# An encoder block's output projection in seven half-size products per half of K, with its stages passed through DRAM

## The chip, the cores and the metric

One core of a Trainium2 chip runs the whole program. The metric is device microseconds of one execution. TensorE (PE) multiplies matrices into PSUM, eight banks of 128 x 512 float32. VectorE (DVE), ScalarE (ACT) and GpSimd (POOL) work on tiles of 128 partitions. Each engine takes its instructions in order. All transfers are issued by SyncE (SP), in order too, and run on 16 DMA engines.

## The reference

```python
h = rmsnorm(x, norm_w[l])                              # x: (1, 1024, 2048)
proj = jnp.einsum('bsd,de->bse', h, w_in[l])           # 2048 -> 5632
q_a, k_a, v_a, g_a, q_r, k_r, v_r, g_r = jnp.split(proj, points, axis=-1)
attn = windowed_attention(q_a, k_a, v_a, sink, rel_bias)   # 16 heads of 64, 4 kv heads, blocks of 128, +-128 tokens
attn = rmsnorm(attn, attn_out_norm_w[l]) * jax.nn.silu(g_a)
qr, kr = rotary(q_r), rotary(k_r) * RET_KEY_DIM ** -0.5
ret = bidirectional_retention(qr, kr, vr, decay_fwd, decay_bwd)   # 8 heads, chunks of 128
ret = head_groupnorm(ret, ret_gn_w[l]) * jax.nn.silu(g_r)
mixed = jnp.concatenate([attn, ret], axis=-1)          # (1, 1024, 2048)
x = x + jnp.einsum('bse,ed->bsd', mixed, w_out[l])     # 2048 -> 2048
return rmsnorm(x, final_norm_w)
```

## The kernel before

Every float32 operand of a large matmul is split into a high and a low part of the type that TensorE takes in one pass (`split`: ScalarE writes the high part, another engine the rest), and each product is three matmuls: high x high, high x low, low x high.

**Input projection.** `UNITS` lists 22 blocks of 256 columns: `ka`, `va` (keys and values of the attention), `qa` 0 to 3, `ga` and `gr` (gates), and for each pair of retention heads `qk` and `vr`. A unit is 16 steps over k, each with 12 matmuls of 128x512 (24 of 128x256 for `va` and `vr`) into four PSUM banks; at the last k the banks are evicted (`evac`) into tiles. The weights of two k-steps come in one tile, loaded a pair ahead (`w_load`) and split a pair ahead (`w_split`).

**What runs between.** After each bank's matmuls of a k-step the code calls `point()`, which lets generators emit a piece of other work. `jobs` holds the attention of four head groups (`attn_job`), then the retention of four pairs (`ret_job`); `aux` holds the setup, the row norms (`sumsq`), the relative-bias rows (`bias_rows`), the decays, and the work that follows a unit (gates, rotation). The order that the generators give is the program's order on every engine and on SP. `drain` runs a generator to a named end at once.

**Tiles.** `t2` is a pool of six tiles of 128x512, `t4` of five of 128x1024. Gates (`gd`), attention and retention outputs (`md`), keys, bias rows (`bd`) and decays go through DRAM already; q, the values and the rotated q and k of the retention stay on the chip.

**Output projection.** K is the 2048 mixed features. Blocks are 512 tokens (`hf`) x 512 columns (`cb`), four banks of 128 tokens, 16 steps over k with 12 matmuls of 128x512: 8 blocks. Rows of `md` are loaded, weighted, split into `hT` (`mixed_row`). `evac_out` adds x to a bank, `finish_out` applies the final norm to four tiles of 128 tokens, `finish_last` to the last.

```python
                for b in range(4):
                    p = banks[b]
                    mh, ml = row[:, 128 * b : 128 * b + 128], row[:, 512 + 128 * b : 512 + 128 * b + 128]
                    T.matmul(p, mh, wh, start=(k == 0), stop=False)
                    T.matmul(p, mh, wl, start=False, stop=False)
                    T.matmul(p, ml, wh, start=False, stop=(k == NK - 1))
```

Of the kernel before, what the change touches and what calls it, by code (L numbers as in the profile page):

```python
# [21 lines left out]
W_IN_TILES = 22 * 8  # L22

UNITS = [("ka", 0), ("va", 0), ("ga", 0), ("qa", 0)]
UNITS += [("ga", 1), ("gr", 0), ("qa", 1), ("ga", 2), ("gr", 1), ("qa", 2), ("ga", 3), ("qa", 3), ("gr", 2)]
for _p in range(4):
    UNITS += [("qk", _p), ("vr", _p)]
UNITS += [("gr", 3)]
TOK_MAJOR = ("va", "vr")
# [3 lines left out]
def hybrid_block(ctx: ExitStack, tc: tile.TileContext, a: dict, out: bass.AP):  # L33
# [5 lines left out]
    md = dram.tile([2048, S], F32, name="md")  # L39
    kd = dram.tile([256, S], F32, name="kd")  # L40
    vd = dram.tile([4, 128, 8, 64], F32, name="vd")
    bd = dram.tile([16, 128, 512], F32, name="bd")
    br = dram.tile([16, 512], F32, name="br")
    dd = dram.tile([8, 128, 128], F32, name="dd")
    qdd = dram.tile([4, 128, 2, 128], F32, name="qdd")
    rbd = dram.tile([128, S], F32, name="rbd")

    cp = ctx.enter_context(tc.tile_pool(name="const", bufs=1))
    wp = ctx.enter_context(tc.tile_pool(name="w", bufs=2))
    hp = ctx.enter_context(tc.tile_pool(name="h", bufs=1))  # L50
    ps = ctx.enter_context(tc.tile_pool(name="ps", bufs=1, space=PSUM))
    com_ctx = ctx.enter_context(ExitStack())
    com = com_ctx.enter_context(tc.tile_pool(name="com", bufs=1))
    ph_ctx = ctx.enter_context(ExitStack())
    att = ph_ctx.enter_context(tc.tile_pool(name="att", bufs=1))

    hT = hp.tile([128, 32, 1024], F32R, name="hT")
# [8 lines left out]
    rb = cp.tile([128, S], F32, name="rb")  # L66
# [4 lines left out]
    phase = [att]  # L71
# [5 lines left out]
    def t4(dt=F32):  # L77
        return com.tile([128, 1024], dt, tag="t4", name=nm("t4_"), bufs=5)

    def t2():  # L80
        return com.tile([128, 512], F32, tag="t2", name=nm("t2_"), bufs=6)
# [7 lines left out]
    def pS():  # L89
        return psum("S", 2)  # L90

    def pT():
        return psum("T", 1)

    def pO():
        return psum("O", 1)

# [10 lines left out]
    def rsqrt_small(v, k, tag, bufs=1):  # L108
        y = small(k, tag + "y", bufs)
        t = small(k, tag + "t", bufs)  # L110
        tt(G, y, v, mhalf[:, :k], ALU.pow)
        tt(V, t, v, y, ALU.mult)
        tt(V, t, t, y, ALU.mult)
        V.tensor_scalar(t, t, -0.5, 1.5, ALU.mult, ALU.add)
        return y, t

    def col_to_rows(col, dst):
        for h in range(2):
            p = pS()
            for i in range(4):  # L120
                c = 4 * h + i
                T.matmul(
                    p[:, 128 * i : 128 * i + 128],
                    col[:, c : c + 1].to_broadcast([128, 128]),
                    ident,
                    start=(i == 0),
                    stop=True,
                    skip_group_check=True,
                )
            A.copy(dst[:, 512 * h : 512 * h + 512], p)  # L130


    wraw, wsp, wide = {}, {}, [None]

    def w_src(i):
        return a["w_in"][i] if i < W_IN_TILES else a["w_out"][(i - W_IN_TILES) % 64]

    n_w = W_IN_TILES + 112

    def w_load(i):  # L140
        if i < n_w and i not in wraw:
            r = wp.tile([128, 512], F32, tag="wr", name=f"wr{i}")
# [3 lines left out]
    def w_split(i):  # L146
        if i < n_w and i not in wsp:
            if wide[0] is None or i % 2:
                hi = wp.tile([128, 512], F32R, tag="wh", name=f"wh{i}")
                lo = wp.tile([128, 512], F32R, tag="wl", name=f"wl{i}")  # L150
            else:
                hi = wide[0].tile([128, 512], F32R, tag="wh", name=f"wh{i}", bufs=2)
                lo = wide[0].tile([128, 512], F32R, tag="wl", name=f"wl{i}", bufs=2)
            r = wraw.pop(i)
            split(hi, lo, r, G if i < W_IN_TILES else V)
            wsp[i] = (hi, lo)


    jobs, aux = deque(), deque()
# [20 lines left out]
    pt, due, pace, apace = [0], [0], [3], [2]  # L180

    def point():
        pt[0] += 1
        if pt[0] >= due[0]:
            due[0] = max(due[0], pt[0] - 1) + pace[0]
            pump(jobs, 1)
        if pt[0] % apace[0] == 0:
            pump(aux, 1)

    def drain(queue, until):  # L190
        while until not in done:
            if until is None and not queue:
                return
# [7 lines left out]
    xraw = {}  # L201
# [9 lines left out]

    def x_split(k):
        if k < NK:
            r = xraw.pop(k)
            n = nw[:, k : k + 1]
            for z in (0, 512) if k == 0 else (0,):
                sl = slice(z, z + 512) if k == 0 else slice(0, 1024)
                if k:
                    A.activation(hT[:, 2 * k, sl], r[:, sl], AF.Copy, scale=n)
                else:  # L220
                    V.tensor_scalar(hT[:, 2 * k, sl], r[:, sl], n, None, ALU.mult)
                stt(V, hT[:, 2 * k + 1, sl], r[:, sl], n, hT[:, 2 * k, sl].bitcast(F32), ALU.mult, ALU.subtract)

    def setup():
# [5 lines left out]
        V.tensor_scalar(ew, ew, 0.5, None, ALU.mult)  # L230
# [3 lines left out]
    def bias_rows():  # L234
# [11 lines left out]
        SP.dma_start(br, bt[:16, :])  # L246
        yield
        reps = {}
        for h in range(16 + 1):
            if h < 16:  # L250
                reps[h] = t2()
                b0 = br[h : h + 1, 0:512]
                SP.dma_start(reps[h], bass.AP(tensor=b0.tensor, offset=b0.offset, ap=[[0, 128], [1, 512]]))
            if h:
                SP.dma_start(bd[h - 1], reps.pop(h - 1))
            yield
        done.add("bias")

    def sumsq():
# [20 lines left out]
        for _ in range(7):  # L280
            yield
        col_to_rows(rcol, rb)
        done.add("rb")
        yield

    def decay():
# [37 lines left out]
        ab = t2()  # L324
        SP.dma_start(ab, a["masks"])
        yield
        yield
        for h in range(8):
            o = t2() if h % 4 == 0 else o
            oo = o[:, 128 * (h % 4) : 128 * (h % 4) + 128]  # L330
            V.tensor_scalar(oo, ab[:, 0:128], lg[:, h : h + 1], None, ALU.mult)
            stt(V, oo, ab[:, 128:256], lg[:, 8 + h : 9 + h], oo, ALU.mult, ALU.add)
            A.activation(oo, oo, AF.Exp)
            V.tensor_scalar(oo, oo, 0.125, None, ALU.mult)
            SP.dma_start(dd[h], oo)
            yield
        for p in range(4):
            o = t2() if p % 2 == 0 else o
            oo = o[:, 256 * (p % 2) : 256 * (p % 2) + 256]
            A.activation(oo[:, 0:128], ab[:, 256:384], AF.Exp, scale=lg[:, 16 + p : 17 + p])  # L340
            A.activation(oo[:, 128:256], ab[:, 384:512], AF.Exp, scale=lg[:, 20 + p : 21 + p])
            SP.dma_start(qdd[p], oo.rearrange("p (d i) -> p d i", d=2))
            yield
        done.add("decay")


    def k_post(tiles):
        while "rb" not in done:
            yield
        for b, t in enumerate(tiles):  # L350
            et, hf = b // 2, b % 2
            stt(V, t, t, 0.125, rb[:, 512 * hf : 512 * hf + 512], ALU.mult, ALU.mult)
            SP.dma_start(kd[128 * et : 128 * et + 128, 512 * hf : 512 * hf + 512], t)
            yield
        done.add("k")

    def gate_post(tiles, et0, key, late=None):
        for b, g in tiles:
            et, hf = b // 2, b % 2

            e = t2()
            A.activation(e, g, AF.Tanh, scale=0.5)
            yield
            stt(V, g, e, 1.0, g, ALU.add, ALU.mult)
            c = et0 + et
            if late is None:
                SP.dma_start(gd[128 * c : 128 * c + 128, 512 * hf : 512 * hf + 512], g)
            else:
                yield
                while ("ret", 3) not in done:  # L370
                    yield
                late(et, hf, g)
            yield
        done.add(key)

    def rope_post(p, tiles, rq, rk):
        for hf in range(2):
            cs, sn = (retp[0].tile([128, 512], F32, tag="mr", name=nm("cs"), bufs=2) for _ in range(2))
            SP.dma_start(cs, a["cos"][:, 512 * hf : 512 * hf + 512])
            SP.dma_start(sn, a["sin"][:, 512 * hf : 512 * hf + 512])  # L380
            yield
            for et, dst in ((0, rq), (1, rk)):
                t = tiles[2 * et + hf]
                sh = t2()
                V.stream_shuffle(sh, t, [i ^ 1 for i in range(32)])
                tt(V, t, t, cs, ALU.mult)
                yield
                tt(V, sh, sh, sn, ALU.mult)
                tt(V, dst[:, 512 * hf : 512 * hf + 512], t, sh, ALU.add)
                yield  # L390
        done.add(("rope", p))
# [4 lines left out]
    def attn_job(g, q_tiles, start):  # L396
        pace[0] = (4.5, 4.5, 3, 3.8)[g]
        kh, kl, vs = t4(F32R), t4(F32R), t4(F32R)
        bias = {}
# [5 lines left out]

        load_bias(0)
        load_bias(1)
        for hf in range(2):
            kr = t2()
            for d2 in range(2):  # L410
                SP.dma_start(kr[64 * d2 : 64 * d2 + 64, :], kd[64 * g : 64 * g + 64, 512 * hf : 512 * hf + 512])
            split(kh[:, 512 * hf : 512 * hf + 512], kl[:, 512 * hf : 512 * hf + 512], kr)
        yield
        vr = t2()
        SP.dma_start(vr, vd[g].rearrange("p t d -> p (t d)"))
# [666 lines left out]
```

## Time and profile before

| what | value |
|---|---|
| median of three runs | 1583.9 us (1580.77 to 1584.82) |
| the profiled execution | 1581.46 us, its span 1579.7 us |
| TensorE busy | 1539.7 us, 97% |
| VectorE, ScalarE, GpSimd busy | 798.9, 525.2, 414.1 us |
| DMA | 171.76 MB, mean 109 GB/s |
| mean granted TensorE clock | 0.994 |

Times in the views are microseconds from the span's start. A group's row gives line, engine, operation, tiles written and read, shape, count, then busy time, mean of one in ns, and the engine's idle time before it with what ended it. In a chain, "start, length, what" stand in a row. TensorE's matmuls are pipelined: each is shown longer than the distance to the next.

### The profile page before, as it was taken

The page shows a single profiled execution, that of the slowest core. Times are in us where ns is not written, and L with a number is a line of the kernel's source. Part 1 is how long each engine was busy: PE and PEld are TensorE (multiplying, and loading weights), DVE is VectorE, ACT ScalarE, POOL GpSimd, SP SyncE. Part 2 cuts the span into 40 slices and gives each one's busy share as a digit, 9 for nine tenths or more (in the row PEclk, how much of TensorE's full clock was granted, in tenths as well). Part 3 has the DMA queues.
Part 4 walks back from the last instruction along what each step waited for, and adds up shares of the span by engine and source line. Part 5 has one row for each costly group of instructions (what it writes and reads, how often), then busy time and mean ns, then how long its engine had stood idle before and what let it go on. Part 6 is the DMA issues. An engine that isn't in the chain of part 4 may idle for free.

```text
span 1579.7 us, 22620 instructions
## 1 busy us (share of the span) xinstructions
PE 1539.7 (97%) x8338; PEld 1327.6 (84%) x8338; DVE 798.9 (51%) x1888; ACT 525.2 (33%) x1186; POOL 414.1 (26%) x435
## 2 busy tenths in 40 slices
PE   8979999999999999999999999999999999999997
PEld 6968888888888888888998998998988888888886
DVE  5511156644656478466534825735567463463323
ACT  5412145543554356456410111111123243433310
POOL 2212223332334334334331423323322000320000
PEclk9989999999999999999999999999999999999999
DMA  8774313131213123212231321312222565675423
GB/s 299 246 248 125 104 43 92 51 114 45 84 56 114 48 60 94 73 48 83 54 113 41 107 61 50 111 41 67 88 89 91 186 205 151 180 247 139 127 61 113
DMA packets 111020, 171.76 MB, mean 109 GB/s; under 512 B 17932, under 2 KB 39436, under 8 KB 110781
## 3 DMA queue, kind: packets, MB, share of 16 engines
q1 hardware_dynamic: 110908, 170.32, 35.3%
q8 instruction: 65, 1.06, 0.3%
q14 instruction: 47, 0.38, 0.1%
HBM read 138.26 MB, written 32.01 MB: 108 GB/s over the span
## 4 chain that ended last, share of the span: by engine, by line
PE 82%; DVE 8%; DMA 4%; issue 3%; ACT 1%; POOL 1%; SPq 0%; POOLq 0%; ACTq 0%; DVEq 0%
PE psM L817 14%; PE psM L818 14%; PE psM L819 14%; PE psM L811 3%; PE psM L812 3%; PE psM L810 3%; PE psM L900 3%; PE psM L901 3%; PE psM L899 3%; PE psT L502 2%; DMA t<-br 1%; DVE t L102 1%; PE psS L900 1%; PE psS L899 1%; PE psS L901 1%
## 5 line engine op out<-in xcount | busy, mean ns | idle before, releaser
L817 PE MATMUL psM<-hT,wh 128*128 128x512 f32 x1088 | 443.0, 407 | 14.9 <-ACT t L741 8.7
L819 PE MATMUL psM<-hT,wl 128*128 128x512 f32 x1088 | 425.9, 392 | 2.0 <-POOL wl L99 2.0
L818 PE MATMUL psM<-hT,wh 128*128 128x512 f32 x1088 | 426.2, 392 | 0.0
L99 POOL TENSOR_TENSOR wl<-wr,wh 128x512 fp32r<-128x512 f32 x176 | 234.5, 1333 | 583.7 <-ACT wh L105 570.7
L105 ACT CAST wh<-wr 128x512 fp32r<-128x512 f32 x288 | 178.5, 620 | 568.7 <-PE psM L818 226.4
L817 PEld LDWEIGHTS psM<-hT,wh 128*128 128x128 f32 x1088 | 205.7, 189 | 53.6 <-ACT t L741 8.9
L819 PEld LDWEIGHTS psM<-hT,wl 128*128 128x128 f32 x1088 | 204.9, 188 | 47.3 <-POOL wl L99 2.4
L818 PEld LDWEIGHTS psM<-hT,wh 128*128 128x128 f32 x1088 | 206.1, 189 | 37.5 <-DVE hT L102 0.7
L810 PE MATMUL psM<-wh,hT 128*128 128x256 f32 x640 | 183.5, 287 | 1.4 <-ACT wh L105 1.4
L811 PE MATMUL psM<-wl,hT 128*128 128x256 f32 x640 | 181.9, 284 | 2.4 <-POOL wl L99 2.4
L812 PE MATMUL psM<-wh,hT 128*128 128x256 f32 x640 | 181.8, 284 | 0.0
L99 DVE TENSOR_TENSOR wl<-wr,wh 128x512 fp32r<-128x512 f32 x112 | 84.1, 751 | 130.8 <-ACT wh L105 130.7
L811 PEld LDWEIGHTS psM<-wl,hT 128*128 128x128 f32 x640 | 123.4, 193 | 3.0 <-POOL wl L99 2.8
L810 PEld LDWEIGHTS psM<-wh,hT 128*128 128x128 f32 x640 | 123.5, 193 | 2.5 <-ACT wh L105 1.6
L812 PEld LDWEIGHTS psM<-wh,hT 128*128 128x128 f32 x640 | 123.4, 193 | 0.0
L450 DVE CUSTOM_DVE_ANT_0 P<-psS,bias,nsink 128x384 f32<-128x384 f32 (+1 forms) x128 | 74.3, 580 | 91.7 <-PE psS L444 91.3
L454 ACT ACTIVATE P<-P,nmx 128x384 f32<-128x384 f32 (+1 forms) x128 | 75.6, 590 | 92.1 <-DVE nmx L450 90.7
L900 PE MATMUL psM<-wl,hT 128*128 128x512 f32 x256 | 100.0, 391 | 0.6 <-DVE wl L99 0.5
L899 PE MATMUL psM<-wh,hT 128*128 128x512 f32 x256 | 100.0, 391 | 0.0
L901 PE MATMUL psM<-wh,hT 128*128 128x512 f32 x256 | 99.7, 389 | 0.0
L99 POOL TENSOR_TENSOR acc<-acc,sq 64x128 f32<-64x128 f32 x112 | 54.9, 490 | 156.2 <-ACT sq L483 148.1
L99 DVE TENSOR_TENSOR t<-psM,rb 128x512 f32<-128x512 f32 x64 | 42.2, 685 | 93.4 <-PE psM L819 93.2
(200 smaller groups left out, 2259.6 us busy)
## 6 DMA issues: line engine op xcount, KB each, us to landing
wr<-in_w_in SPq DMA_DIRECT2D x176, 256.0 KB, 2.7
wr<-in_w_out SPq DMA_DIRECT2D x112, 256.0 KB, 2.8
t<-in_x SPq DMA_DIRECT2D x16, 512.0 KB, 6.9
mr<-md SPq DMA_DIRECT2D x32, 256.0 KB, 3.0
xr<-in_x SPq DMA_DIRECT2D x32, 256.0 KB, 3.9
out<-y SPq DMA_DIRECT2D x32, 256.0 KB, 3.0
t<-in_xT SPq DMA_DIRECT2D x15, 512.0 KB, 5.8
gd<-t SPq DMA_DIRECT2D x28, 256.0 KB, 2.4
```

The source lines that it names most:

```text
L99: eng.tensor_tensor(o, x, y, op)
L105: A.copy(o_hi, x)
L454: A.activation(x[:, :W], x[:, :W], AF.Exp, bias=nmx[:, c : c + 1], scale=-1.0, accum_out=sums[:, c : c + 1])
L810: T.matmul(po, hh[:, sl], wh[:, ws], start=first and z == 0, stop=False, skip_group_check=True)
L811: T.matmul(po, hh[:, sl], wl[:, ws], start=False, stop=False, skip_group_check=True)
L812: T.matmul(po, hl[:, sl], wh[:, ws], start=False, stop=last, skip_group_check=True)
L817: T.matmul(p, wh[:, ws], hh[:, sl], start=first, stop=False)
L818: T.matmul(p, wh[:, ws], hl[:, sl], start=False, stop=False)
L819: T.matmul(p, wl[:, ws], hh[:, sl], start=False, stop=last)
L899: T.matmul(p, mh, wh, start=(k == 0), stop=False)
L900: T.matmul(p, mh, wl, start=False, stop=False)
L901: T.matmul(p, ml, wh, start=False, stop=(k == NK - 1))
```

## The change

**The output projection** is now four problems: half of K (`f`) x half of the columns (`u`, 1024). In each, the mixed features are a matrix of 2 x 2 quarters of 512 tokens x 512 features, the weights 2 x 2 quarters of 512 x 512, and the four quarters of the result come from seven products of one (sums or differences of) feature quarters with one of weight quarters (Strassen's scheme in the form with shared sums). A product is 4 k-steps x 4 token tiles x 3 matmuls of 128x512 in four banks; a product's banks are added to tiles of the result, some products run on in the banks of another.

- `w_combine` makes the four weight combinations of each (`f`, `u`, k) during the input units and stores them in `wd`.
- `premix` reads a row of `md` and its gate from `gd`, weights it and writes it back to `md`; `combine` reads four quarters, makes four combinations and stores them in `cd`. Those of `f` = 0 are made during units 15 to 20, those of `f` = 1 during the first seven products. `c_load` and `c_split` bring the operand rows into `H`, seven tiles that hold the normed input before.
- `e_load` brings x (for `f` = 0) or the partial result `yd` (for `f` = 1) into tiles, `e_done` stores the partial result or squares the final one, `finish` and `finish_last` apply the final norm.

**The stages** pass through DRAM: q's parts (`qsd`), both halves of the attention's sum (`mpd`, added by `attn_sum`), rotated q and k (`rqk`), values (`vrd`). The units' order is new (all gates last), a store is issued some points after its data is made (`store`), the sink is a further column of the exponential's row, and gates use SiLU instead of tanh. **The bias rows** are copied for one head group at a time (`bias_copies`), group 0 before unit 2, the rest from unit 5 on.

```diff
+W_OUT = [
+    (f, u, p, j)
+    for f in range(2)
+    for u in range(2)
+    for p in ((0, 1, 2, 3, 6, 4, 5) if f and u else (0, 1, 2, 3, 4, 6, 5))
+    for j in range(4)
+]
...
+    def t2(dt=F32):
+        return out_of(com, [128, 512], dt, "t2", NT2)
...
-        for h in range(16 + 1):
+    def bias_copies(g):
+        yield ready("rows")
+        for h in range(4 * g, 4 * g + 4):
+            r = t2()
+            b0 = br[h : h + 1, 0:512]
+            SP.dma_start(r, bass.AP(tensor=b0.tensor, offset=b0.offset, ap=[[0, 128], [1, 512]]))
+            yield
+            yield
+            store(bd[h], r, r, (lambda: done.add(("bias", g))) if h % 4 == 3 else None, 1)
+            yield
...
+    def premix(kk):
+        for hf in range(2):
+            sl = slice(512 * hf, 512 * hf + 512)
+            r, g = t2(), t2()
+            SP.dma_start(r, md[128 * kk : 128 * kk + 128, sl])
+            SP.dma_start(g, gd[128 * kk : 128 * kk + 128, sl])
...
+            yield
+            yield
+            stt(V, r, r, ew[:, kk : kk + 1], g, ALU.mult, ALU.mult)
+            store(md[128 * kk : 128 * kk + 128, sl], r, r, (lambda: done.add(("pre", kk))) if hf else None, 2)
...
+    def combine(f, j):
+        yield ready(("pre", 8 * f + j), ("pre", 8 * f + 4 + j))
+        q = [t2() for _ in range(4)]
+        for n in (0, 2, 3, 1):
+            SP.dma_start(q[n], q_mix(f, j, n))
...
+        c = t2()
+        tt(V, c, q[0], q[2], ALU.subtract)
+        store(cd[f, 2, j], c, c, None, 2)
...
+    for j in range(4):
+        for kk in (8 + j, 12 + j):
+            aux.append((premix(kk), None))
+        if j:
+            aux.append((combine(1, j - 1), None))
+    aux.append((combine(1, 3), None))
+    apace[0] = 1.3
...
+        def products(j, t):
+            wh, wl = wsp[W_STD + 4 * n + j]
+            hh, hl = (H[p][:, j, 512 * z + 128 * t : 512 * z + 128 * t + 128] for z in range(2))
+            fresh = j == 0 and p in (0, 1, 3)
+            T.matmul(banks[t], hh, wh, start=fresh, stop=False, skip_group_check=True)
+            T.matmul(banks[t], hh, wl, start=False, stop=False, skip_group_check=True)
+            T.matmul(banks[t], hl, wh, start=False, stop=(j == 3), skip_group_check=True)
+
+        def stream(i):
+            w_split(i + 1)
+            w_load(i + 2)
+            w_load(i + 3)
```

How the instructions stand now, at three places. The transfers on SP ahead of the eviction of unit 1 (`va`, stored to `vd`), before: copies of bias rows out of `br` into `t2` tiles and on to `bd`, with the weights (`wr`) between.

```order
L255 DMA bd<-t_65_891 128x512
L253 DMA t_66_906<-br 128x512
L253 DMA t_67_921<-br 128x512
L255 DMA bd<-t_66_906 128x512
L255 DMA bd<-t_67_921 128x512
L143 DMA wr_943<-in_w_in 128x512
L253 DMA t_69_957<-br 128x512
L255 DMA bd<-t_68_936 128x512
L253 DMA t_70_972<-br 128x512
L745 DMA vd<-t_71_981 128x4x64
```

The same place now: the last of group 0's four copies, the decays' columns (`dc`, `jc`), and loads and stores of weight combinations (`wc`, `wd`).

```order
L113 DMA bd<-t_123_930 128x512
L370 DMA t_127_988<-br 128x512
L113 DMA wd<-wc_852 128x512
L244 DMA wc_1053<-in_w_out 128x512
L412 DMA dc_1058<-in_ret_decay_bwd 64x4x1 x2
L417 DMA jc_1065<-in_jcol 128x2
L113 DMA wd<-wc_928 128x512
L113 DMA bd<-t_127_988 128x512
L228 DMA wc_1177<-in_w_out 128x512
L113 DMA vd<-t_128_1002 128x4x64 x2
```

Twelve of the sixteen copies have left this place; the decays' gathers, which stood behind the copies, stand among the last of them.

SP at the start of the output projection, before: weights (`wr`), feature rows from `md` (`mr`), x (`xr`).

```order
L143 DMA wr_12202<-in_w_out 128x512
L143 DMA wr_12227<-in_w_out 128x512
L893 DMA fw<-in_final_norm_w 128x2048
L143 DMA wr_12251<-in_w_out 128x512
L946 DMA xr_12333<-in_x 128x512
L143 DMA wr_12272<-in_w_out 128x512
L946 DMA xr_12342<-in_x 128x512
L946 DMA xr_12351<-in_x 128x512
L714 DMA mr_12404<-md 128x512
L143 DMA wr_12295<-in_w_out 128x512
```

Now, in the third product: weights (`e`, from `wd`), `premix` (L845, L846, its store L113 to `md`), `combine` (L867, stores to `cd`), the partial result (`yd`).

```order
L113 DMA md<-t_2191_12257 128x512
L214 DMA e_2200_12297<-wd 128x512
L867 DMA t_2201_12303<-md 128x512
L867 DMA t_2203_12305<-md 128x512
L113 DMA md<-t_2196_12278 128x512
L867 DMA t_2204_12306<-md 128x512
L867 DMA t_2202_12304<-md 128x512
L214 DMA e_2207_12324<-wd 128x512
L113 DMA yd<-acc_12108 128x512
L113 DMA cd<-t_2208_12330 128x512
L113 DMA cd<-t_2203_12305 128x512
L113 DMA yd<-acc_12110 128x512
```

Between two loads of weights stood one or two other transfers; now there are four or five.

TensorE in the output projection, before, one k-step's last tile and the next step's first: a tile has 16 such steps.

```order
L899 MATMUL psM_11927<-wh_12128,hT 128x512
L900 MATMUL psM_11927<-wl_12129,hT 128x512
L901 MATMUL psM_11927<-wh_12128,hT 128x512
L899 MATMUL psM_11924<-wh_12154,hT 128x512
L900 MATMUL psM_11924<-wl_12155,hT 128x512
L901 MATMUL psM_11924<-wh_12154,hT 128x512
```

Now, in the first product: the same three matmuls, operand rows from `H`, and the scheduler has put a tile's second k-step ahead of the next tile's first.

```order
L1210 MATMUL psMa_12116<-wh_12035,h0r 128x512
L1211 MATMUL psMa_12116<-wl_12036,h0r 128x512
L1212 MATMUL psMa_12116<-wh_12035,h0r 128x512
L1210 MATMUL psMa_12116<-wh_12132,h0r 128x512
L1211 MATMUL psMa_12116<-wl_12133,h0r 128x512
L1212 MATMUL psMa_12116<-wh_12132,h0r 128x512
```

The form of a matmul is unchanged; a product takes 48 of them, and there are 28 products.

More of the change, by code (lines that the diff above doesn't have):

```diff
@@ L70, in hybrid_block @@
     cnt = [0]
[L71 removed]
+    phase = [stp]
     def nm(p):
@@ L191, in drain @@
         while until not in done:
-            if until is None and not queue:
-                return
+            if not queue:
+                flush(True)
+                if until is None or until in done:
+                    return
             g, _ = queue[0]
@@ L407, in attn_job @@
         load_bias(1)
[L408 to L417 removed]
+        q_load(0)
```

1082 lines of the change are left out of this document (617 added, 465 removed).

## The prediction

> **What bounds the kernel now.** I read the page's busy shares and the chain first, then the steps of the matmuls in time, then what TensorE waits for, then stretches of the span with the DMA share beside them.
>
> ```profile
> span 1579.7 us, 22620 instructions
> PE 1539.7 (97%) x8338; PEld 1327.6 (84%) x8338; DVE 798.9 (51%) x1888; ACT 525.2 (33%) x1186; POOL 414.1 (26%) x435
> PE 82%; DVE 8%; DMA 4%; issue 3%; ACT 1%; POOL 1%; SPq 0%; POOLq 0%; ACTq 0%; DVEq 0%
> ```
>
> TensorE is busy for all but 40 us, and it holds 82% of the chain that ended last: what it need not do comes off the time, as long as it is fed. Busy matmuls overlap, so the mean of one (389 ns) is not its price. The price is the distance of the starts:
>
> ```profile
> 1308.38 0.39 PE L899 MATMUL psM<-wh,hT 128*128 128x512 f32 x1
> 1308.61 0.39 PE L900 MATMUL psM<-wl,hT 128*128 128x512 f32 x1
> ...
> 1309.74 0.39 PE L899 MATMUL psM<-wh,hT 128*128 128x512 f32 x1
> ```
>
> Six starts in 1.36 us: 0.227 us for one 128x512 matmul. What TensorE waits for, and where (in the rows of stretches the columns are length, busy time of PE, PEld, DVE, ACT and POOL with counts, granted clock, DMA share, GB/s):
>
> ```profile
> PE psM L817 <- ACT t L741: 8.7, 1, 8.7
> PE psM L817 <- DVE hT L221: 6.2, 1, 6.2
> ...
> 35.00:40.00 5.00, 5.00 (x24) 4.14 (x23) 2.22 (x4) 2.93 (x4) 1.72 (x1) 1.00 1.03 409
> 160.00:820.00 660.00, 653.92 (x3455) 560.92 (x3454) 363.88 (x942) 301.08 (x778) 232.52 (x280) 1.00 0.26 75
> 820.00:1217.00 397.00, 390.54 (x2538) 351.38 (x2537) 218.20 (x545) 58.77 (x103) 117.06 (x94) 1.00 0.24 75
> 1217.00:1293.00 76.00, 75.52 (x349) 62.42 (x348) 45.09 (x94) 30.47 (x57) 2.86 (x2) 1.00 0.57 184
> 1400.00:1420.00 20.00, 19.91 (x88) 16.15 (x87) 16.53 (x39) 3.83 (x7) 2.02 (x3) 1.00 0.88 288
> 92.00:116.00 24.00, 12.99 (x83) 12.09 (x82) 1.75 (x4) 2.70 (x6) 3.08 (x3) 0.79 0.91 281
> 40.00:60.00 20.00, 20.00 (x121) 17.89 (x119) 11.96 (x15) 9.62 (x16) 4.07 (x3) 1.00 0.98 346
> 1217.00:1570.00 353.00, 352.44 (x1568) 291.00 (x1566) 157.19 (x286) 112.14 (x215) 27.68 (x25) 1.00 0.51 156
> 1570.00:1579.70 9.70, 0.09 (x1) 0.00 (x0) 3.19 (x11) 2.24 (x6) 0.92 (x1) 0.69 0.32 108
> ```
>
> So the idle time is the head (6.2), one hole near 105 us, 6.1 us in the attention stretch (160 to 820), 6.5 in the retention stretch (820 to 1217), under 1 us in the output projection, and 9.7 after the last matmul. The output projection uses half of the DMA engines' time. The rows 40:60 and 35:40 show how fast they go when they are asked for everything: 346 GB/s over 20 us, 409 over 5.
>
> **The products.** Before: 8 blocks x 16 k x 4 tiles x 3 = 1536 matmuls of 128x512. After: 4 (half of K, half of the columns) x 7 products x 4 k x 4 tiles x 3 = 1344. All other matmuls stay in number and shape. 192 x 0.227 = **-43.6 us**. That is all that arithmetic can give; the sums and differences that pay for it go to VectorE and the DMA engines.
>
> **The start.** The 16 bias rows are now copied for one head group (4 rows) before the attention opens, the rest later. Before, all 16 went through the six `t2` tiles in one go, and the eviction of `va` waited for a free one:
>
> ```profile
> 84.37 5.39 DMA t<-br
> 90.14 4.11 DMA t<-br
> ...
> 103.86 4.82 DMA t<-br
> 108.70 4.60 DMA bd<-t
> 113.48 0.85 ACT t L741 x2
> 114.37 0.80 PE psM L817
> ```
>
> and in the timeline (start, duration, line, tiles):
>
> ```profile
> 114.97 0.63 PE L818 MATMUL psM<-hT,wh 128*128 128x512 f32 x1
> 115.39 0.63 PE L819 MATMUL psM<-hT,wl 128*128 128x512 f32 x1
> ```
>
> Row 92:116 has 24.0 - 13.0 = 11.0 us of idle TensorE, and then matmuls start 0.42 to 0.43 us apart (114.97, 115.39) instead of 0.227; I count 12 of them up to 119.7, 2.4 us. Together 13.4. With 4 copies between `br` and `vd` in place of 16 the hole goes; late next is the decay's column of small gathers, which lands after 6 to 7 us:
>
> ```profile
> dc<-in_ret_decay_bwd SPq DMA_DIRECT2D x2, 1.0 KB, 7.0
> jc<-in_jcol SPq DMA_DIRECT2D x1, 1.0 KB, 6.6
> ```
>
> VectorE waits for it just ahead of the same eviction: 0 to 4 us, I take 1.4. Sum **-12** (-13 to -9).
>
> **Attention and retention.** q, k, v, the attention's sums and the rotated q and k now go through DRAM, so the engines do less per step. Per head step VectorE loses half of the scaling (L462), the q parts and the sum of the two halves:
>
> ```profile
> L462 DVE TENSOR_SCALAR P<-P,sums 128x384 f32<-128x384 f32 x96 | 46.1, 523 | 1.5
> L99 DVE TENSOR_TENSOR qj<-t,qj 64x256 fp32r<-64x256 f32 x64 | 30.5, 476 | 1.9
> L99 DVE TENSOR_TENSOR u<-psO,sq 64x256 f32<-64x256 f32 x64 | 26.6, 415 | 61.6 <-ACT sq L479 60.1 <-POOL wl L99 0.7 <-issue 0.6
> ```
>
> About 0.26 + 0.24 + 0.21 of some 2.3 us. TensorE's 12.6 us of idle time in these two stretches are what less work there can win; new are loads that an engine can wait for in order, with 42 to 69 DMAs in each of the units 2 to 7 where there were 14 to 34. At 60% use of the DMA engines a load lands in about the time of the rows below (3 to 4 us) and stands two to three steps ahead of its use. I take **-4** (-10 to +15). The 64 differences of weights (0.69 us each, L947's price below) run beside the input projection on a VectorE that row 160:820 has at 55%; one more table load for the gates' SiLU is 1.3 us on ScalarE behind banks that VectorE frees. Both cost nothing as long as the DMAs land; with that cover gone they are in the upper bound.
>
> **The output projection's feed.** This is the term that decides. The combinations of the first half of K are made during the last input units, those of the second half during the first seven products: 8 rows x 2 halves x 3 DMAs (read `md` and `gd`, write `md`) = 48, four combinations x 8 = 32, weights 28, x tiles in 20, partial y out 16, the last gates 4: 148 DMAs of 256 KB, 38.8 MB, in 7 x 48 x 0.227 = 76.3 us of matmuls. That asks for 509 GB/s; row 1217:1293, the same 76 us before, has 184.
>
> ```profile
> wr<-in_w_out SPq DMA_DIRECT2D x112, 256.0 KB, 2.8
> mr<-md SPq DMA_DIRECT2D x32, 256.0 KB, 3.0
> xr<-in_x SPq DMA_DIRECT2D x32, 256.0 KB, 3.9
> L964 SPq DMA_DIRECT2D out<-y x28: 332/332/454, 1399.5 to 1565.3; - x28
> L947 DVE TENSOR_TENSOR y<-psM,xr 128x512 f32<-128x512 f32 x19 | 12.6, 687 | 32.4 <-PE psM L928 15.4 <-DMA xr<-in_x 9.5 <-PE psM L901 7.5
> ```
>
> The weights of a step stand in the same SP queue as all these, three k-steps (8 us) ahead, so TensorE follows the queue. Issuing is not the limit (148 x 0.33 = 49 us). At 409 GB/s the 38.8 MB take 95 us, at 346 they take 112, at the 281 of row 92:116 they take 138. I take 346, the longest stretch near a full share: 112 - 76 = **+36** (19 to 62). The second seven products carry 95 DMAs, 24.9 MB: 72 us at 346, 76 by row 1400:1420 scaled to a full share (288 / 0.88 = 327). That just fits: **+3** (0 to 12). The last fourteen carry little.
>
> The Trainium skill, "DMA: Bandwidth & Descriptors", Specifications, gives about 358 GB/s as the HBM limit of one core; by that figure the stretch would take 108 us, an estimate 4 us below my term. The 409 of row 35:40 stands above that figure, so the measurement decides, and my lower bound stays.
>
> **Change of stage and tail.** At the end of the last input unit ScalarE and VectorE split rows whose loads were issued one k-step (12 x 0.227 = 2.7 us) before and land in 3.0; the banks of the first product are freed by VectorE behind them: **+4** (0 to 10). At the end, three scalings of the third tile on ScalarE (0.71 us each, L994) stand ahead of the last tile's squares:
>
> ```profile
> L994 ACT ACTIVATE y<-y,fy 128x512 f32<-128x512 f32 x2 | 1.3, 714 | 2.0 <-DVE fy L989 2.0
> ```
>
> **+2** on the 9.7 (0 to 8).
>
> **Sum.** The profiled execution took 1581.5 us for its span of 1579.7. 1581.5 - 43.6 - 12 - 4 + 36 + 3 + 4 + 2 = 1566.9. The median of the three runs, 1583.9, is 2.4 above that execution, so 1569 beside the median.
>
> **Rivals.**
>
> *The feed is hidden.* The queue reaches the best rate (409), or the splits' order lets part of it go early: feed +19 or less, the rest as above: 1552; with the smaller terms at their good ends 1537. For it: 409 and a share of 1.03 in row 35:40. Against: those are loads alone, and a third of the new traffic is stores. Chance 0.2.
>
> *Round trips through six tiles (slower).* `premix` and `combine` take all their tiles from `t2`, six of them: load, VectorE, store, and the next load waits until the store has landed. That is the chain of 84 to 113 us, where six tiles gave 281 GB/s at a share of 0.91 and one DMA in the chain took 4 to 5 us. Place: the first seven products. 38.8 MB at 281 is 138 us, feed +62: 1595. Without the feed the sum is -50.6, so it decides from 127 us for the seven products (306 GB/s) on: above, the change gains nothing. For it: the same tiles and the same pattern; against: weights and x tiles have buffers of their own and fill the queue. Chance 0.2.
>
> *Half clock.* If the waits come in pieces as long as the hole at 105 us, matmuls go on at 0.43 us: 336 x 0.43 = 144 us, feed +68: 1601. For it: rows 114.97 and 115.39; against: the need is spread, about 1.3 us of waiting for each of 28 k-steps, and a 6.2 us head is the only other long wait. Chance 0.07. The Trainium skill, "TensorE: Matmul & The Clock Gate", Part 1, says the same: after an idle window of some 3.4 us the clock halves until it has been busy as long. The trace agrees (0.43 after 8.7 us).
>
> *The change does not cut the work*, because what it takes off TensorE comes back as reloads or extra passes: TensorE's instructions are 192 fewer in the order, so 0.03.
>
> **How the numbers follow.** My forecast (feed between the rates 409 and 306) has 0.5, its own range 1552 to 1582. Less than 0.3% (4.8 us) can hardly be told from no change in this kernel, whose three runs span 4.0 us. Faster (below 1579): all of the hidden case, most of mine, 0.66. Same: the upper end of mine and the lower of the round trips, 0.13. Slower: 0.21. The range 1540 to 1597 leaves out the best of the hidden case and the half clock.
>
> **What would show it.** Right: first seven products in 105 to 120 us, DMA share above 0.9 there, TensorE waiting for ScalarE's or GpSimd's split of weights that wait for the DMA; fourteen last products at 10.9 us each; no hole before 120 us; 1344 matmuls at 0.227. Wrong: seven products in under 95 us (feed over-counted) or over 127 (round trips); slow steps of 0.43 in the output; a hole in attention units 5 to 7, where 45 to 69 DMAs of a unit now stand in one queue. Most likely to fail is the rate at which a mix of loads and stores with VectorE in between can go.

## The result: 4.3% slower, where 1% faster was forecast

The changed kernel takes 1652.8 us (median; 1644.8 to 1656.2) against 1583.9 before: ratio 1.0431, 95% interval 1.0388 to 1.0475. The page after, its span, TensorE's busy time and the chain:

```profile
span 1648.1 us, 23052 instructions
PE 1537.3 (93%) x8146; PEld 1307.5 (79%) x8146; DVE 760.7 (46%) x1745; ACT 567.7 (34%) x1226; POOL 420.9 (26%) x337
PE 53%; DMA 9%; DVE 5%; POOL 2%; SPq 2%; issue 2%; ACT 1%; POOLq 0%; ACTq 0%; DVEq 0%
```

TensorE holds 53% of the chain instead of 82%, transfers 9% instead of 4%. The program moves 318.10 MB where it moved 171.76. Stretches after (columns as before): units 5 to 8, 9 to 13, 14 to 21, the first and the second seven products, and what follows the last matmul:

```profile
244.80:512.60 267.80, 246.16 (x1425) 215.59 (x1423) 139.25 (x383) 119.21 (x301) 49.80 (x39) 0.97 0.58 182
512.60:816.90 304.30, 294.50 (x2036) 276.28 (x2034) 144.16 (x411) 132.37 (x329) 81.72 (x62) 0.98 0.44 135
816.90:1270.70 453.80, 436.74 (x2178) 361.13 (x2177) 193.22 (x463) 130.12 (x256) 154.19 (x125) 0.99 0.50 165
1270.70:1404.30 133.60, 99.85 (x336) 69.65 (x337) 46.22 (x65) 20.77 (x34) 36.55 (x29) 0.87 0.87 289
1404.30:1480.50 76.20, 76.20 (x338) 63.07 (x337) 38.29 (x58) 32.45 (x56) 34.55 (x26) 1.00 0.92 315
1634.90:1648.10 13.20, 0.00 (x0) 0.00 (x0) 4.62 (x18) 5.79 (x12) 1.47 (x2) 0.59 0.85 289
```

The span grew by 68.4 us: the start (to the end of unit 2) 160.5 to 154.4, -6.1; units 3 to 21, 1056.2 to 1116.3, +60.1; the output projection 353.3 to 364.2, +10.9; what follows it +3.5. So the gain in products was eaten in the output projection, and as much again was lost in the input units, where only small effects were expected.

How an input unit loses time, on VectorE, then TensorE, then GpSimd (start, length, instruction, in brackets the idle time before it and what ended it):

```profile
416.15 0.08 DVE L588 DVE_READ_ACCUMULATOR2_ANT nmx<- 128x1 f32 x1
421.71 0.69 DVE L160 TENSOR_TENSOR t<-t,e 128x512 f32<-128x512 f32 x1 [5.48 <-DMA e<-in_sin]
422.32 0.16 DVE L564 RECIPROCAL sums<-sums 128x2 f32<-128x2 f32 x1
424.12 0.69 PE L625 MATMUL psST<-ident,P 128*128 128x128 f32 x2 [5.30 <-DVE nmx L588]
415.30 1.54 POOL L160 TENSOR_TENSOR wl<-e,wh 128x512 fp32r<-128x512 f32 x1 [5.09 <-ACT wh L166]
416.80 1.28 POOL L160 TENSOR_TENSOR t<-t,e 128x512 f32<-128x512 f32 x1
```

and on SP in the same microseconds:

```profile
411.79 0.32 SPq L113 DMA_DIRECT2D rqk<-t  x1
416.86 0.33 SPq L214 DMA_DIRECT2D e<-in_w_in  x1
418.10 0.33 SPq L503 DMA_DIRECT2D e<-in_sin  x1
```

VectorE is idle for 5.48 us ahead of a multiplication of the rotation whose sine rows are not there. They go into the one tile that the cosine rows stand in (tag `e22`, a single buffer), so SP could issue their load only at 418.10, when GpSimd's multiplication by the cosine (416.80 to 418.08) had read it; and GpSimd came to that late, behind a weight split ahead of which it was idle for 5.09 us. The kernel before loaded cosine and sine together, into two tiles. The softmax of the attention waits behind VectorE's multiplication, and TensorE behind the softmax. VectorE's longest waits for loads between 200 and 820 us:

```profile
DVE wc L160 <- DMA wc<-in_w_out: 50.7, 22, 4.9
DVE t L160 <- DMA e<-in_sin: 28.5, 13, 5.5
DVE t L160 <- DMA t<-mpd: 27.7, 8, 4.8
```

### The profile page after: what moved, and what is told of

Read it like the earlier page. It is cut to its first block, busy times and chain, and to the rows that moved or that the text cites. A ratio compares the mean times of both kernels' runs of the same rounds, so it can differ in the third digit from the quotient of the medians.

```text
span 1648.1 us, 23052 instructions
## 1 busy us (share of the span) xinstructions
PE 1537.3 (93%) x8146; PEld 1307.5 (79%) x8146; DVE 760.7 (46%) x1745; ACT 567.7 (34%) x1226; POOL 420.9 (26%) x337
## 2 busy tenths in 40 slices
DMA packets 195024, 318.10 MB, mean 193 GB/s; under 512 B 29995, under 2 KB 59691, under 8 KB 194268
## 4 chain that ended last, share of the span: by engine, by line
PE 53%; DMA 9%; DVE 5%; POOL 2%; SPq 2%; issue 2%; ACT 1%; POOLq 0%; ACTq 0%; DVEq 0%
PE psMb L1043 4%; PE psMa L1043 4%; PE psMa L1045 4%; PE psMb L1044 4%; PE psMb L1045 4%; PE psMa L1044 4%; DMA t<-gd 2%; DMA t<-rbd 2%; PE psST L625 2%; PE psST L1210 2%; PE psST L1212 2%; PE psST L1211 2%; PE psMa L1211 1%; PE psMb L1038 1%; PE psMb L1037 1%
## 5 line engine op out<-in xcount | busy, mean ns | idle before, releaser
L160 POOL TENSOR_TENSOR wl<-e,wh 128x512 fp32r<-128x512 f32 x232 | 308.7, 1332 | 898.0 <-ACT wh L166 862.9
L166 ACT CAST wh<-e 128x512 fp32r<-128x512 f32 x288 | 178.0, 618 | 523.5 <-PE psMb L1044 137.8
L588 DVE CUSTOM_DVE_ANT_0 P<-psST,bias,nsink 128x384 f32<-128x384 f32 (+1 forms) x128 | 74.2, 581 | 81.7 <-PE psST L580 81.7
L160 DVE TENSOR_TENSOR wc<-wc,wc 128x512 f32<-128x512 f32 x64 | 51.1, 798 | 120.5 <-DMA wc<-in_w_out 112.1
L592 ACT ACTIVATE P<-P,nmx 128x385 f32<-128x385 f32 (+1 forms) x128 | 75.9, 593 | 66.0 <-DVE nmx L588 64.8
L160 DVE TENSOR_TENSOR PTl<-psST,PTh 128x384 fp32r<-128x384 f32 (+1 forms) x128 | 66.8, 522 | 52.2 <-ACT PTh L632 49.2
L160 DVE TENSOR_TENSOR t<-t,t 128x512 f32<-128x512 f32 (+1 forms) x80 | 64.0, 803 | 56.4 <-DMA t<-mpd 34.8
L632 ACT CAST PTh<-psST 128x384 fp32r<-128x384 f32 (+1 forms) x128 | 57.7, 451 | 74.6 <-PE psST L625 74.1
L625 PE MATMUL psST<-ident,P 128*128 128x128 f32 x352 | 60.1, 275 | 9.4 <-DVE nmx L588 6.7
L610 PE MATMUL psO<-PTh,k 128*128 128x256 f32 x176 | 45.4, 283 | 3.7 <-ACT PTh L632 3.7
L579 PE MATMUL psST<-k,qj 128*128 128x384 f32 (+1 forms) x128 | 41.5, 325 | 1.7 <-DVE PTl L160 1.7
L611 PEld LDWEIGHTS psO<-PTl,k 128*128 128x128 f32 x176 | 33.5, 191 | 11.9 <-DVE PTl L160 10.7
L580 PE MATMUL psST<-k,qj 128*128 128x384 f32 (+1 forms) x128 | 41.6, 325 | 0.0
L610 PEld LDWEIGHTS psO<-PTh,k 128*128 128x128 f32 x176 | 33.6, 191 | 4.1 <-ACT PTh L632 3.9
L1043 PE MATMUL psMa<-h0r,wh 128*128 128x512 f32 x60 | 25.5, 427 | 8.9 <-DVE h0r L335 6.2
```

The source lines that it names most:

```text
L160: eng.tensor_tensor(o, x, y, op)
L166: A.copy(o_hi, x)
L588: V.tensor_tensor_reduce(x[:, :W], p[:, :W], bias[2 * pr + c][:, k0 : k0 + W], -1.0, nsink[:, head : head + 1], ALU.add, ALU.min, nmx[:, c ...
L592: A.activation(x[:, : W + 1], x[:, : W + 1], AF.Exp, bias=nmx[:, c : c + 1], scale=-1.0, accum_out=sums[:, c : c + 1])
L610: T.matmul(o[:, :256], vs3[:, m0 + i, :], hi[:, i, :, :], start=(i == 0), stop=False)
L611: T.matmul(o[:, :256], vs3[:, m0 + i, :], lo[:, i, :, :], start=False, stop=(i == m1 - m0 - 1))
```

## The experiments

Units are counted off by their matmuls in the trace. The time in the second column is a median; the columns behind it are of one profiled execution, which lies 7.4 us above the median for e2, 10.1 above it for e6 and 7.4 below it for e7, so a difference of a few us between two columns shows little. "Less" and "more" in the text compare the medians, each beside the kernel before on its own chip. Excess is a stretch's length less its matmuls at their step (512 columns 0.227 us, 384 0.176, 256 0.119, 128 0.11). "7 a", "7 b" are the first and second seven products.

| run | us | kernel before, same chip | units 0-2 | 3-4 | 5-8 | 9-13 | 14-21 | 7 a | 7 b |
|---|---|---|---|---|---|---|---|---|---|
| before | 1583.9 | | 19.3 | 0.1 | 4.5 | 8.3 | 17.7 | | |
| after | 1652.8 | 1583.9 | 13.1 | 3.2 | 32.4 | 17.1 | 34.7 | 57.5 | 0.0 |
| e1_ahead | 1663.0 | 1582.7 | 13.6 | 4.9 | 21.9 | 15.0 | 46.8 | 64.5 | 0.0 |
| e2_no_wsum | 1619.1 | 1582.7 | 4.3 | -0.2 | 13.7 | 19.1 | 36.0 | 61.5 | 0.0 |
| e3_no_f1_sums | 1603.5 | 1582.7 | 12.0 | 5.9 | 28.8 | 18.2 | 35.4 | 9.9 | 0.0 |
| e4_all_rows | 1650.9 | 1582.7 | 15.3 | 10.3 | 24.3 | 17.7 | 33.8 | 57.8 | 0.0 |
| e5_r_tiles | 1634.3 | 1581.7 | 12.2 | 3.0 | 31.9 | 17.7 | 40.2 | 38.4 | 0.0 |
| e6_spread | 1632.9 | 1581.7 | 11.8 | 7.7 | 28.1 | 21.3 | 36.4 | 33.6 | 11.8 |
| e7_fused | 1617.0 | 1581.7 | 11.1 | 7.8 | 27.9 | 14.1 | 32.8 | 23.5 | 0.0 |
| e8_wsum_late | 1649.3 | 1581.7 | 6.6 | 3.6 | 33.2 | 20.3 | 35.7 | 60.2 | 0.0 |
| e9_wsum_held | 1638.2 | 1582.4 | 3.4 | -0.2 | 14.5 | 36.3 | 33.9 | 57.2 | 0.0 |
| e10_norm_row | 1650.4 | 1582.4 | 10.4 | 5.8 | 32.1 | 15.4 | 33.1 | 61.5 | 0.0 |
| e11_three | 1608.0 | 1582.4 | 11.9 | 7.9 | 24.3 | 21.3 | 28.1 | 25.4 | 0.0 |
| e12_no_f0_sums | 1637.9 | 1582.5 | 12.8 | 4.9 | 32.8 | 18.0 | 21.0 | 56.8 | 0.0 |
| e13_wsum_pool | 1672.7 | 1582.5 | 24.8 | 19.5 | 30.7 | 14.3 | 34.9 | 62.1 | 0.0 |
| e14_fused_pool | 1642.6 | 1582.5 | 21.4 | 20.8 | 30.1 | 18.0 | 31.7 | 24.3 | 0.0 |
| e15_no_sums | 1553.2 | 1581.1 | 3.6 | -0.2 | 13.4 | 20.6 | 18.6 | 9.6 | 0.0 |
| e16_fused_held | 1608.0 | 1581.1 | 3.9 | -0.2 | 13.4 | 41.9 | 34.7 | 25.5 | 0.0 |

### Which sums cost what: three parts left out, then all

> The changed kernel without the weight sums: no loads, differences and stores of the combinations during the input units, the products read plain quarters of the weights instead (64 loads, 64 stores, 64 VectorE instructions of 0.8 us left out; the result of the products is another). Theory A: VectorE waited 51 us for these loads between 200 and 820 us; units 5 to 8 lose most of their excess of 32 us, the time falls by 20 (10 to 30) to about 1633; units 11 to 21 and the output stay. Rival B (volume): the same units lose as much, but also the start (units 1 to 4). Rival D (the rotation and the sum of the halves alone make the holes): within 6 us of 1653.

```diff
-    slow.append((w_combine(0), 16))
-    slow.append((w_combine(1), None))
```

1619.1: 32.5 less beside the kernel before on its chip (36.4 above it instead of 68.9). Units 5 to 8 lose 18.7 of their excess, the start and units 3 to 4 another 12, as only the rival of volume had it. In the profiled execution the columns fall by 24 us in all, so the size is known to some us only. And the run takes out the loads, the stores and VectorE's waits together: it shows what the sums cost, not by which of these.

> The changed kernel without the weighting and the sums of the second half of K: the products of that half read unweighted quarters (left out: 80 of the 148 transfers of the first seven products, 24 VectorE instructions of weighting and 16 sums). If the transfers set the pace (theory of the prediction), 68 transfers, 17.8 MB, fit in 76 us and the excess of the output, 58 us, falls under 10: about 1603. If the split of weights on GpSimd (1.33 us for each of 28) or the change of stage sets it, 20 us or more of excess stay: 1615 to 1650.

```diff
-    aux.append((combine(1, 3), None))
...
-            drain(aux, ("comb", 1, 3))
```

1603.5, 48.1 less; 9.9 of excess stays, 9.9 of it in the first product (the change of stage). Neither the split on GpSimd nor the order of the splits sets the pace; the weighting and the sums do, their 80 transfers and their VectorE work together.

> The changed kernel without the weighting and the sums of the first half of K (made during units 15 to 21; its products read unweighted quarters). Left out: 48 loads, 16 stores of the weighting with 16 GpSimd and 16 VectorE instructions, 16 loads, 16 stores, 16 differences of the sums. If this work makes the loss of the retention stretch (excess 35 us against 18 before the change), units 15 to 21 fall to 14 to 22 of excess: time 1634 (1628 to 1642). If the retention's own new loads and stores make it: above 1645.

```diff
-                    aux.append((after(premix(c), ("ga", c // 2)), None))
-                    aux.append((combine(0, j), None))
```

1637.9, 13.5 less, all in units 14 to 21.

> The changed kernel without any sums: no weight sums, no weighting and no sums of either half of K (e2, e3 and e12 together; the products read plain quarters). If the three effects add (32.5, 48.1 and 13.5 us, each against the kernel before on its own chip): 94 us less, 1559 (1552 to 1566), below the kernel before. If they overlap (a stretch that waits for one also waits for another): 1570 or more.

1553.2: 27.9 us under the kernel before (ratio 0.9813, 0.9791 to 0.9834), 96.8 less than the change. The three parts add (94.1), so the sums are the loss: they cost 97 us and 79.8 MB of transfers (238.34 MB are left). The half-size products without them would be a gain.

### The first seven products

> The changed kernel; the weighting and the sums of the second half of K, during the first seven products, take their tiles from the eight of the tag r instead of the six t2 (which the loads of the next operands and the squares keep). Same instructions and transfers, fewer of them wait for a tile's store. Theory of round trips: the seven products, 134 us, fall to 112 (rate 346) or below, the time by 20 or more, to about 1632. Theory of the rate (a mix of loads and stores goes at 290 GB/s however many tiles it has): within 6 us of 1653.

```diff
-            r, g = t2(), t2()
+            r, g = side[0](), side[0]()
...
+    side[0] = r2
```

From the output stage on, `side[0]` gives the eight `r` tiles.

> The changed kernel with the sums of the second half of K spread over ten products instead of seven (all weighting first, then the sums, 2.3 steps apart instead of 1.3; awaited before the loads for the product that needs them). Same transfers. Theory of peaks (waits between load, sum, store set the pace, and more time covers them): output excess falls from 58 to 25 to 40 us, time about 1625 to 1640. Theory of volume (189 transfers, 49.5 MB, in the first ten products, 109 us, at 290 to 327 GB/s): excess 42 to 62, time 1637 to 1657.

```diff
-    apace[0] = 1.3
+    apace[0] = 2.3
```

The sums also stand behind all of the weighting, and are awaited in the tenth product, ahead of the loads that need them.

> The changed kernel; weighting and sums of the second half of K made in one go: four quarters and gates loaded into four r and four t2 tiles, weighted, summed, stored (60 transfers instead of 80, the same VectorE work, no read of what was just written). By volume at 290 GB/s the first seven products take 33.6 MB / 290 = 116 us instead of 134: time about 1635; by round trips (one fewer in each chain, and twelve tiles more) they take 95 to 105: about 1618.

```diff
-            aux.append((premix(kk), None))
...
+        aux.append((mix_combine(j), None))
```

`mix_combine` loads, weights and sums four quarters, with eight loads and seven stores.

The first seven products of e3, e5, e6 and e7, in this order (last column GB/s):

```profile
1270.50:1356.70 86.20, 80.80 (x337) 65.83 (x338) 22.88 (x33) 20.83 (x34) 37.02 (x29) 0.94 0.72 229
1275.30:1389.90 114.60, 93.26 (x336) 68.77 (x337) 38.92 (x57) 21.02 (x35) 37.54 (x29) 0.90 0.89 296
1275.50:1385.30 109.80, 89.69 (x336) 66.41 (x337) 41.64 (x57) 19.52 (x32) 34.94 (x27) 0.93 0.91 305
1264.10:1363.90 99.80, 86.70 (x336) 67.84 (x337) 52.25 (x65) 20.52 (x34) 41.43 (x29) 0.92 0.89 313
```

Unit 21 and the first seven products belong together here, so this is unit 21 of the change and of e5:

```profile
1213.70:1270.70 57.00, 53.39 (x275) 44.69 (x274) 37.30 (x87) 29.85 (x59) 19.01 (x16) 1.00 0.66 222
1211.90:1275.30 63.40, 55.71 (x275) 45.93 (x274) 41.14 (x95) 29.42 (x58) 18.45 (x15) 0.97 0.83 275
```

e5 fell by 16.3 us, nearer to the theory of round trips (20 or more) than to that of the rate (within 6), though not by a better rate in the seven products: 296, nearly the 289 of the change. With tiles free earlier, 129 transfers instead of 148 are issued in them, and the other 19 in unit 21, which took 6 us longer. Both stretches together carry the same volume, 51.3 MB in the change and 51.4 in e5 (length x rate, added), in 190.6 and 178.0 us. So with the volume unchanged more tiles won 12.6 us. That is clear of what these products vary by in the runs that leave them and their operands alone (56.8 to 62.1 us of excess).

e6 decides nothing: its median, 1632.9, lies where the theory of peaks had it; in its profiled execution, which was its slowest (1643.0), the excess is 33.6 + 11.8 = 45.4, as the theory of volume had it, because 5 MB moved into the next seven products.

e7's 99.8 us and 1617.0 are what the round trips gave (95 to 105, 1618) and not what the volume gave (116, 1635). But e7 changes both: its stretch carries 31.2 MB instead of 38.6, at 313 instead of 289. So the volume and the waits for tiles both count, and how the 57.5 us divide between them is not shown.

The rate stays under the 346 of row 40:60 in all four. An estimate from the DMA shares of these rows: at a full share the change would have 289 / 0.87 = 332 and row 40:60 346 / 0.98 = 353. So about two thirds of the gap is time in which the DMA engines were idle. In the change SP stood there 18.9 us for weighted rows that it was to store and 12.0 for sums; in e5 8.9 and 8.8. What the rest of the gap is, the mix of loads and stores or another thing, stays open.

### The input units

> The changed kernel with more steps between the issue of a side load and its first use: cos 3 to 8 steps, sin 6 to 12, the attention halves 3 to 6, gates and norm rows of the first half of K 2 to 5, weight quarters 2 to 4 (of the slow queue). The same instructions on every engine. Theory A (VectorE, GpSimd and ScalarE stand in order for a side load that was issued too late, and softmax or the weight split stands behind it): the excess of units 5 to 21, 84 us, falls by 25 to 50, the time to about 1615 (1600 to 1630). Rival B (the volume of the transfers is what slows the input units): within 8 us of 1653. Rival C (longer lives of the six tiles make new waits): above 1660.

```diff
-            for _ in range(6):
+            for _ in range(12):
```

These are the steps between the load of the sine and its use. 1663.0, 11.4 more and not less, in the range of rival C. Units 5 to 8 win 10 us and units 14 to 17 13.6, as theory A said, but units 18 to 21 lose 25.8: the sums of the first half of K, now slower, were not done when the last unit needed them (the last store was issued at 1242.9 us; before this edit at 1142.4, 71 us ahead of unit 21). Whether longer lives of the tiles slowed them or the added steps themselves is not shown.

> The changed kernel with the weight sums begun at unit 9 instead of unit 1, where the DMA engines are at 0.3 to 0.5 of their time. Same instructions. If crowding of the first eight units made the loss (16 us in units 0 to 4, 19 in 5 to 8): units 0 to 8 as without the sums, units 9 to 18 lose 0 to 12 more, time 1620 to 1635. If VectorE's wait for a load in order is what costs, wherever it stands: the loss moves with the sums and the time stays within 8 us of 1653.

```diff
-    slow.append((w_combine(0), 16))
+    slow.append((w_combine(0), 16 * 9))
```

1649.3. The first difference ran at 85.0 us instead of 62.9, far ahead of unit 9. So a sentence in the description above is wrong: the order of the generators is a priority, and these loads, which depend on nothing, were set ahead of it. This also means that a number of steps in the code is no distance on the engine.

> The changed kernel; the three tiles of the weight sums are held, by a read that needs a bank of unit 8, so that no load of the sums can be issued before unit 9 (the earlier try by the emission step alone moved them by 22 us only: loads without a dependency were set earlier in SP's order). Crowding of units 1 to 8 as cause: they get as fast as without the sums (31 us less up to unit 8), units 9 to 18 lose up to 12: time 1630 (1620 to 1640). The wait in order as cause: units 9 to 18 lose 15 to 30, time 1640 to 1660.

```diff
+    held = [wc_() for _ in range(3)]
...
+                    if (u, b) == (9 - 1, 0):
+                        for x in held:
+                            tt(V, ones[:, 1:2], x[:, 0:1], st[0][:, 0:1], ALU.add)
```

Units 5 to 8 and 9 to 13 of e9:

```profile
231.70:481.70 250.00, 241.10 (x1423) 214.29 (x1422) 124.55 (x361) 119.61 (x301) 50.06 (x40) 0.99 0.48 148
481.70:805.30 323.60, 299.63 (x2037) 277.90 (x2036) 182.97 (x475) 133.02 (x329) 81.48 (x62) 0.98 0.73 231
```

1638.2, 13.1 less. The units without the sums are as fast as in e2; units 9 to 13, whose matmuls are the same, lose 19.2, above the 12 that crowding was given. The time is in the range of crowding (1620 to 1640), the loss of units 9 to 13 in that of the wait in order (15 to 30), so the two are not told apart. The loss goes where the sums go; in a place that was less busy (DMA share 0.44 in units 9 to 13 of the change, 0.58 in its units 5 to 8) it is smaller.

> The changed kernel with the 64 differences of the weight sums on GpSimd instead of VectorE; the same transfers. GpSimd takes 1.3 us for one where VectorE takes 0.8, and splits the weights a pair of steps (5.4 us) ahead. Theory A (softmax stands on VectorE behind the wait for a load): units 5 to 8, excess 32 us, lose 10 to 19 of it: time 1640 (1632 to 1645). If the transfers themselves (crowding, the order of SP) make the loss: within 6 us of 1653. If the weight split now stands behind the loads: above 1660.

```diff
-                tt(V, y, x, y, ALU.subtract)
+                tt(G, y, x, y, ALU.subtract)
```

1672.7, 21 us more than the change. TensorE's and GpSimd's waits (to 280 us, and from 40 to 450 us):

```profile
PE psST L1045 <- POOL wl L160: 14.0, 6, 4.6
POOL wc L160 <- DMA wc<-in_w_out: 78.6, 23, 10.5
```

VectorE no longer waits for the quarters, GpSimd does, with the split of weights behind it. Units 0 to 4 have 28 us more of excess. Units 5 to 8 keep 30.7 of their 32.4, so the 10 to 19 that theory A gave them back are not there: either the transfers make that loss, or GpSimd's waits took the place of VectorE's. An engine that is idle three quarters of its time was no cover for a wait in order.

> The changed kernel with the two halves of the attention's norm row loaded once into two tiles of the weight sums (free by then) instead of 16 loads into t2 tiles. 14 transfers and 16 uses of the six tiles fewer, all else the same. In the chain of the changed kernel the loads of this row that GpSimd waits for (with the weight split behind them) stand for 1.7% of the span, 28 us, of which a part is covered: theory A (in-order wait for a late load) gives units 15 to 21, excess 35 us, 10 to 20 back: time 1638. Rival (retention itself is as slow as before the change, 18 us of excess of its own, and other loads take the place): within 6 us of 1653.

```diff
-                n = t2()
+                if hf not in norm_row:
+                    norm_row[hf] = wc_()
```

1650.4, 0.9 less beside the kernel before: the loads that the chain named were gone, and the excess of units 14 to 21 stayed at 33.1. The chain then ran through the next loads:

```profile
870.93 6.43 DMA t<-md
886.99 4.30 DMA t<-gd
```

> The changed kernel with all 16 bias rows copied at the start, as before the change. The hole of 9 us at 105 us comes back: units 1 and 2 take 8 to 12 us more; the 12 copies that then are missing in units 5 to 7 give 0 to 8 back. Theory: 1656 (1650 to 1664). If the start was won by something else than the grouping: units 0 to 2 stay at 148 us.

```diff
-    aux.append((bias_copies(0), None))
+    for g in range(4):
+        aux.append((bias_copies(g), None))
```

1650.9, no difference to the change, and the hole at 105 us did not come back. But the copies did not come back to that place either: SP issued four loads out of `br` by 90.3 us, the other twelve from 112.4 to 179.5, behind the end of unit 1 (102.7), where the kernel before issued all 16 between 83.5 and 112.9, ahead of it (114.4). So the run says nothing about the reason for the hole. The rows cost 7.1 in units 3 to 4 and gave 8.1 back in units 5 to 8.

### A better complete kernel

> e7 and e9 together, complete: weighting and sums of the second half of K in one go, weight sums not before unit 9. If the effects add (34.7 and 13.1 us): 1605 (1598 to 1612), still above the kernel before by 1.4%.

1608.0, as expected: 42 less than the change, still 1.6% above the kernel before. Two more, told in brief: e7 with the norm row of e10 and with cosine and sine of three rotations loaded together into two tiles (e11; 1597 expected, 1588 to 1612) took 1608.0 as well; e7 with e13 (e14; 1604 expected if e13 gained), 1642.6. No complete version beat the kernel before.

## Why the prediction was wrong

**Products, -43.6:** right. 1344 matmuls; the last 21 products take 10.9 us each but for the two at the end.

**Start, -12:** half of it came, -6.1. The hole is gone as forecast (TensorE has no wait over 0.8 us between 74 and 115 us). Without the weight sums (e2) the stretch is 15 us shorter than before, so about 9 of the gain went to those sums. That the copies ahead of the eviction of `va` made the hole fits both kernels, but no run shows it alone, as e4 did not put them back there.

**Attention and retention, -4 (-10 to +15):** this step failed; units 3 to 21 took 60.1 more. That is 64 of the 83 us between the forecast's 1566.9 and the profiled execution's 1649.9. The 64 differences of weights that "run beside the input projection on a VectorE that row 160:820 has at 55%" and "cost nothing as long as the DMAs land" measured 32.5 us (about 9 of it in the start). The sums of the first half of K, not priced in this term at all, measured 13.5. Without any sums 21 us of excess more than before are left in units 5 to 13; the waits for the sine rows and the halves of the attention's sum point there, but no run tried them alone (in e11, with cosine and sine in two tiles, units 5 to 13 keep 45.6 us, in e7 42.0). The warning sign was named, "a hole in attention units 5 to 7", and given no price: VectorE's 45% of idle time was taken for cover, though whatever stands behind a late load in its order is late too. The trace shows such waits (5.48 us above); how much of the 32.5 they make, and how much the crowding by 33.6 MB of transfers more, e9 and e13 leave open.

**Feed, +36 (19 to 62), and change of stage, +4 (0 to 10):** together +57.5. The first product of e3, with the sums of the second half left out, has 9.9, which is the change of stage, at its upper end; some 48 are left for the feed, within its range. The 148 transfers are counted in the trace; the rate was mis-sized, 289 and not 346. The nearest row was 92:116 with 281, which I had taken as the far end. It was also a chain of load and store through the same tiles, and the row at 346 held loads alone. The rival of round trips had this figure, and part of the reason: e5 wins 12.6 us with the same transfers through more tiles. The limit of about 358 GB/s for one core that the Trainium skill gives ("DMA: Bandwidth & Descriptors", Specifications) was not reached in this stretch either.

**Second seven, +3:** 0.0, at 315 GB/s. **Tail, +2:** +3.5, and 2.0 in the last two products. **Half clock** was a part, not a rival: 57 steps of about 0.43 in the first seven products, 11.2 of their 57.5 us.

## What to carry to other kernels

Price a scheme that saves multiplications by its sums first: here seven products in place of eight saved 44 us, and reading, adding and writing the operands cost 97. An engine that is half idle hides work only if nothing that TensorE needs stands behind that work's loads. And take the rate of a transfer-bound stretch from a row with the same kind of chain, not from the best row of loads alone.

## What the runs showed of the hardware

TensorE fell to half clock after shorter waits than the 8.7 us of the trace before:

```profile
1318.28 0.73 PE L1210 MATMUL psMa<-wh,h2r 128*128 128x512 f32 x2 [2.30 <-ACT wh L166]
1319.64 0.63 PE L1211 MATMUL psMa<-wl,h2r 128*128 128x512 f32 x1 [0.39 <-POOL wl L160]
1320.07 0.63 PE L1212 MATMUL psMa<-wh,h2r 128*128 128x512 f32 x1
```

Waits of 2.30 and 0.39 us, close together, and the steps are 0.43; the steps ahead of them were 0.23, and no wait since 1300 us was longer. The Trainium skill ("TensorE: Matmul & The Clock Gate", Part 1) puts one idle window at about 3.4 us, running free of the kernel; where waits are many the trace shows that less than that in one piece is enough.
